# More raw weight buffers, lower priorities for two PE steps, and the attention gate block-transposed with its softmax sums as a row through DRAM

## The chip, the cores and the metric

The kernel runs on one NeuronCore of a Trainium2 chip. The metric is device time in microseconds (us) of one execution; lower is better. The engines are TensorE (PE, with its weight loads as PEld), VectorE (DVE), ScalarE (ACT), GpSimd (POOL) and SyncE (SP), which here only issues DMAs. Each engine works through its own queue in order.

## What is computed

A two-layer backbone over 256 context tokens and 2,048 latent tokens of width 1,024, in float32. Each layer normalises and modulates its input, projects it with one matrix `w_in` into the columns of three head groups, runs the groups, gates each with a SiLU path, and projects the joined result with `w_out` onto the residual. Cut to the part around the change:

```python
xn = _rms_norm(x, g_norm) * (1 + sc) + sh
(au, av, az, bq, bk, bv, bz, cq, ck, cv, co, cz, cg) = _split_proj(xn @ w_in)
...
p = softmax(einsum(q, k) * ATTN_SCALE)        # 8 query heads, 2 key heads, 64 wide
o = einsum(p, v)
y_b = o * silu(bz)                            # the gate z of group B
...
y_a = gelu(au) * (w_s @ layer_norm(gelu(av)) + b_s) * silu(az)
y_c = sigmoid(co) * rms_norm(mlstm forward + mlstm backward) * silu(cz)
x = x + gt * (concatenate([y_a, y_b, y_c]) @ w_out)
```

In the last layer only the latent tokens are put out.

## The kernel before

Tokens are cut into 18 tiles of 128 (2 context, 16 latent), `NT`. Matrix products keep float32 accuracy by splitting each operand into a rounded part and a rest (`F32R`): `split_w` (L214) does it for weights, on ACT and DVE for three chunks in four and on POOL for the fourth, and `gemm` (L223) issues three matmuls for each of the eight chunks `k` of the contraction.

The stages of a layer follow each other as `proj_phase` (L326), `attn_phase` (L1052) and `out_phase` (L229), on one SBUF stack, so that the tiles of one stage lie over the memory of the one before.

**Projection.** The 18 tiles are taken in three macros of six (`half`). For each macro the seven column groups (`groups`, L894: c1, c3, c2, a1, a2, b1, b2) are run one after the other, each over the six tiles. A group's weights are eight chunks of 128 x 512. `wload` (L969) issues their loads into 3 `raw` tiles; `wtick` (L976) splits up to two chunks into a ring of 11 `w` tiles, as far as `freed` allows, which is raised at the half and at the end of the last tile of a group. `tick` (L925) runs after each half of a tile: it advances the generators that are active (epilogues, `make_xn`, the mLSTM) and calls `wtick`. `make_xn` (L474) normalises a tile, transposes it on PE (L497), modulates and splits it; the next macro's tiles are made during the last two groups. `post_a1` (L557) is the gMLP's epilogue with the matmul by `w_s` at L591, and `post_b2` (L672) computes 2 x silu(z) as `z` and stores it to DRAM, tokens in partitions (`g_z`, L142).

**Attention.** A unit is one head and one block of four query tiles (in the first layer also one of the two context tiles), 32 units for the latents in each layer. `unit_s` (L1113) forms the scores on PE, evicts them with a running maximum on DVE (L1126) and exponentiates them on ACT, which also leaves the sums `den`. `unit_tr` (L1137) transposes the probabilities on PE and splits them, every other key tile on ACT and POOL (L1146 to L1148), the others on ACT and DVE. `unit_mm` (L1154) multiplies with the values. A value step is one key tile of a unit, 18 to a unit; the score stream runs about one unit ahead, and the value product follows the transposes by `LAG` = 5 steps.

`unit_end` (L1164) closes a unit at its last value step. For the first head of a pair it loads the gate of both heads, `sz`, with tokens in partitions. DVE takes the reciprocal of `den` (L1174), POOL scales the gate with it, a column of `sz` for each tile (L1176), ACT and DVE add the two halves of the output into `O` (L1180, L1181). At the second head PE transposes the pair's gate, four transposes (L1185), DVE multiplies `O` with it out of PSUM (L1186), and SP stores `O`. The query loads of a unit (`load_twice`, L1079) are four DMAs of pieces of 128 bytes, issued in the middle of the unit before.

**What sets the order.** The program is written out in full, and a scheduler at build time places the instructions of each engine by priority (which falls in the order of writing) in a simulated time. `late(n)` (L60) lowers the priority of what stands under it by n places, `issue_after` and `ld` (L51) order loads on SP.

Of the kernel before, what the change touches and what calls it, by code (L numbers as in the profile page):

```python
# [35 lines left out]
def hybrid_kernel(ctx: ExitStack, tc: tile.TileContext, x, c, ctxt, c_ctx, w_ada, b_ada, g_norm, w_in, w_s, b_s,  # L36
# [105 lines left out]
    g_z = [dram([P, len(b), 512], f"sz{i}") for i, b in enumerate(blocks)]  # L142
# [3 lines left out]
    g_q = [dram([len(b), P, 512], f"sq{i}") for i, b in enumerate(blocks)]  # L146
    g_k = [dram([len(b), P, P], f"sk{i}") for i, b in enumerate(blocks)]
# [178 lines left out]
    def proj_phase(l):  # L326
        with ExitStack() as st:
            xns = slots(st, half + 1, [P, 2, KC, P], "xn", F32R, "right")
            pp, xtp, rawp = (st.enter_context(tc.tile_pool(name=nm(n), bufs=b, reuse_waits="tile"))
                             for n, b in (("post", 2), ("xt", 3), ("raw", 3)))  # L330
            wring = ring(slots(st, 11, [P, 2, 512], "w", F32R))
# [142 lines left out]
            def make_xn(i, slack=True, halves=False):  # L474
# [19 lines left out]
                for b in range(2):  # L494
                    tr = ptr()
                    for k in range(4):
                        T.transpose(tr[:, k * P:(k + 1) * P], xf[:, b * 4 + k, :], ident)  # L497
                    for k in range(4):
                        kk = b * 4 + k
                        if k < 3:  # L500
                            A.activation(xf[:, kk, :], tr[:, k * P:(k + 1) * P], AF.Identity,
                                         scale=modp[l][:, s, 0, kk:kk + 1], bias=modp[l][:, s, 1, kk:kk + 1])
                        else:
                            V.tensor_scalar(xf[:, kk, :], tr[:, k * P:(k + 1) * P], modp[l][:, s, 0, kk:kk + 1],
                                            modp[l][:, s, 1, kk:kk + 1], op0=ALU.mult, op1=ALU.add)
                    bs = slice(b * 4, b * 4 + 4)
                    A.copy(slot[:, 0, bs], xf[:, bs])
                    V.tensor_tensor(slot[:, 1, bs], xf[:, bs], slot[:, 0, bs].bitcast(F32), op=ALU.subtract)
                    if b == 0 and halves:
                        yield  # L510
# [46 lines left out]
            def post_a1(i, acc, full):  # L557
# [29 lines left out]
                for gp in range(2):  # L587
                    yield
                    sv = pm()
                    for q in range(2):  # L590
                        T.matmul(sv[:, q * n:(q + 1) * n], wsT[:, 2 * gp + q, :],  # L591
                                 buf[:, 0, 2 * gp + q, j0:j1, :].rearrange("p t d -> p (t d)"),
                                 start=(q == 0), stop=(q == 1))
                    for q in range(2):
                        zz = buf[:, 1, 2 * gp + q, j0:j1, :].rearrange("p t d -> p (t d)")
                        V.scalar_tensor_tensor(zz, sv[:, q * n:(q + 1) * n], bsT[:, 2 * gp + q:2 * gp + q + 1], zz,
                                               op0=ALU.add, op1=ALU.mult)
# [74 lines left out]
            def post_b2(i, acc, full):  # L672
# [4 lines left out]
                ld(part(g_z, i), z)  # L677
# [291 lines left out]
            def wload():  # L969
                while len(wraw) < len(chunks) and len(wraw) < len(wt) + 3:  # L970
# [5 lines left out]
            def wtick(most=2):  # L976
                for _ in range(most):
                    j = len(wt)
                    if j >= len(chunks) or j >= freed[0] + 11:
                        break  # L980
# [29 lines left out]
            for mi, mac in enumerate(macros):  # L1010
                for gi, (gn, cols) in enumerate(groups):
# [8 lines left out]
                    for ii, i in enumerate(mac):  # L1020
                        full = not (last and i < NCT)
                        ml = mi == NM - 1 and (gi >= 3 or gi == 2 and ii >= 1)
                        if i in todo:
                            acc = pacc()
                            c0, w = (0, n) if full or gn == "c3" else (256, 256)
                            for hf in range(2):
                                gemm(acc, xs[i], ws, c0, w, range(hf * KC // 2, (hf + 1) * KC // 2))
                                if i == todo[-1]:
                                    freed[0] = base + (hf + 1) * KC // 2
                                tick(ml)  # L1030
                                if i == todo[-1]:
                                    wtick()
                            spawn(post[gn](i, acc, full))
# [6 lines left out]
                        if mi + 1 < NM:  # L1040
                            if gi == len(groups) - 2 and ii == half - 2:
                                spawn(make_xn(macros[mi + 1][0]))
                            if gi == len(groups) - 1 and ii + 1 < half:
                                spawn(make_xn(macros[mi + 1][ii + 1]))
# [7 lines left out]
    def attn_phase(l):  # L1052
        last = l == DEPTH - 1
        with ExitStack() as st:
# [109 lines left out]
            def unit_end(u):  # L1164
# [4 lines left out]
                if q == 0:  # L1169
                    sz = pt([P, 4, P], "sz", 3)  # L1170
                    ld(sz[:, 0:n], g_z[b][:, :, u['h'] * HD:(u['h'] + 2) * HD])
                    pairs[b] = sz, pt([P, 512], "O", 3)
                sz, O = pairs[b]
                V.reciprocal(u['den'][:, 0:n], u['den'][:, 0:n])  # L1174
                for j in range(n):
                    G.tensor_scalar(sz[:, j, q * HD:(q + 1) * HD], sz[:, j, q * HD:(q + 1) * HD],  # L1176
                                    u['den'][:, j:j + 1], 0.5, op0=ALU.mult, op1=ALU.mult)
                r = slice(q * 64, q * 64 + 64)
                rx = slice(64 - q * 64, 128 - q * 64)
                A.copy(O[r, 0:w], u['o'][rx, 0:w])  # L1180
                V.tensor_tensor(O[r, 0:w], u['o'][r, 0:w], O[r, 0:w], op=ALU.add)  # L1181
                if q == 1:
                    tr = ptr()
                    for j in range(n):
                        T.transpose(tr[:, j * P:(j + 1) * P], sz[:, j, :], ident)  # L1185
                    V.tensor_tensor(O[:, 0:w], tr[:, 0:w], O[:, 0:w], op=ALU.mult)  # L1186
# [43 lines left out]
            pend = []  # L1230
            sgen = s_stream()
# [26 lines left out]
            def flush(k):  # L1258
                while len(pend) > k:
                    u, s, t = pend.pop(0)  # L1260
                    unit_mm(u, s, t)
                    if s == u['nk'] - 1:
                        unit_end(u)
# [9 lines left out]
            flush(0)  # L1273

# [43 lines left out]
```

## Time and profile before

| | us |
|---|---|
| median of 3 runs | 3688.44 |
| lowest and highest of them | 3686.83, 3696.19 |
| the profiled execution, its own time | 3695.58 |
| its span, first to last instruction | 3693.9 |
| mean granted PE clock, share of full speed | 0.987 |

The runs differ by up to 9 us. The profile is of a single execution: its rows add up to its span of 3693.9 us, with 1.7 us around it, and that execution took 7.1 us more than the median. The stages are, roughly and overlapping: first projection to 905 us, first attention to 1,745, first output projection to 1,945, second projection to 2,690, second attention to 3,510, second output projection to the end. "Busy" of PE counts matmuls from issue to a modelled end, and they overlap. A wait names the engine and line that ended it.

### The profile page before, as it was taken

Reading aid. Unit: us, or ns where it says so; the run is one execution under the profiler, and the core shown is the slowest. Engines: PE = TensorE matmul, PEld = TensorE weight load, DVE = VectorE, ACT = ScalarE, POOL = GpSimd, SP = SyncE. Lnnn points to the kernel's source line nnn. Section 1 sums busy time; section 2 is a strip of 40 time slices with the busy share of each in tenths; the row PEclk is TensorE's granted clock in tenths of the full one; section 3 lists DMA queues with packets and bytes.
Section 4 is the critical chain, followed back from the end, with each engine's and each line's share of the span. In section 5 each row is a group of like instructions: output and inputs, shape, how many; then the busy total and the mean of one; then the engine's idle time right before and its main releaser. Section 6 shows DMA issues by size and latency. Waiting matters only on the chain. (4 is left out here: it accounts for less than half of the span.)

```text
span 3693.9 us, 58457 instructions
## 1 busy us (share of the span) xinstructions
PE 3591.9 (97%) x19405; PEld 2937.9 (80%) x19405; DVE 2564.0 (69%) x6375; ACT 1941.6 (53%) x3443; POOL 1884.4 (51%) x2448
## 2 busy tenths in 40 slices
PE   8999999998999999999999999999999999999999
PEld 4877778776888888887788788877778888888787
DVE  4676664777888888887434636467788888888754
ACT  4223243234877787776114432432368777878621
POOL 2241342453777777776432524245457777777610
PEclk9999999999999999999999999999899999999999
DMA  6446445576111011102645453557710111100143
GB/s 207 137 143 177 138 133 135 167 195 141 26 28 36 14 44 37 24 13 91 181 123 146 130 147 87 139 146 191 172 46 18 29 29 41 30 21 12 58 147 113
DMA packets 567156, 359.20 MB, mean 97 GB/s; under 512 B 348611, under 2 KB 469179, under 8 KB 566853
## 3 DMA queue, kind: packets, MB, share of 16 engines
q1 hardware_dynamic: 553636, 336.04, 34.2%
q0 software_dynamic: 2848, 9.91, 0.8%
q10 hardware_dynamic: 10368, 9.52, 0.8%
q8 instruction: 153, 2.51, 0.3%
q14 instruction: 151, 1.23, 0.1%
HBM read 269.56 MB, written 85.76 MB: 96 GB/s over the span
## 5 line engine op out<-in xcount | busy, mean ns | idle before, releaser
L226 PE MATMUL acc<-w,xn 128*128 128x512 f32 (+2 forms) x4728 | 1097.8, 386 | 7.3 <-ACT w L216 4.5
L226 PEld LDWEIGHTS acc<-w,xn 128*128 128x128 f32 x4728 | 844.8, 191 | 187.4 <-ACT w L216 6.0
L1126 DVE TENSOR_SCALAR_CACHE_REDUCE e<-acc,rqall 128x512 f32<-128x512 f32 (+1 forms) x1296 | 857.0, 688 | 150.3 <-PE acc L1124 86.2
L1159 PE MATMUL m<-pT,vst 128*128 128x512 f32 (+1 forms) x2336 | 775.8, 415 | 3.6 <-POOL pT L1148 3.2
L1124 PE MATMUL acc<-kst,qs 128*128 128x512 f32 (+1 forms) x2592 | 745.9, 385 | 8.2 <-DVE e L1126 7.2
L1148 POOL TENSOR_TENSOR pT<-pf,pT 128x512 fp32r<-128x512 f32 (+1 forms) x564 | 730.0, 1302 | 28.6
L1132 ACT ACTIVATE e<-e,nmx 128x2304 f32<-128x2304 f32 (+1 forms) x272 | 578.2, 2126 | 57.1 <-DVE nmx L1131 56.2
L1147 POOL TENSOR_SCALAR pT<-pf 128x512 fp32r<-128x512 f32 (+1 forms) x564 | 354.0, 632 | 355.8 <-ACT pf L1146 335.6
L1124 PEld LDWEIGHTS acc<-kst,qs 128*128 128x128 f32 x2592 | 446.6, 189 | 86.8 <-DVE e L1126 23.8
L1159 PEld LDWEIGHTS m<-pT,vst 128*128 128x128 f32 x2336 | 412.5, 189 | 66.3 <-POOL pT L1148 9.0
L1141 PE MATMUL tr<-ident,e 128*128 128x128 f32 x3084 | 457.0, 273 | 4.1 <-DVE pT L1151 3.4
L1141 PEld LDWEIGHTS tr<-ident,e 128*128 128x128 f32 x3084 | 373.8, 140 | 81.9 <-DVE pT L1151 6.5
L217 DVE TENSOR_TENSOR w<-raw,w 128x512 fp32r<-128x512 f32 (+1 forms) x276 | 208.1, 765 | 192.1 <-ACT w L216 188.2
L216 ACT CAST w<-raw 128x512 fp32r<-128x512 f32 (+1 forms) x276 | 160.6, 594 | 287.3 <-DMA raw<-in_w_in_dram 259.9
L1151 DVE TENSOR_TENSOR pT<-tr,pT 128x512 fp32r<-128x512 f32 x405 | 273.2, 681 | 52.5 <-ACT pT L1150 51.2
L226 PE MATMUL acc<-w,xs 128*128 128x512 f32 x1224 | 293.3, 397 | 0.6 <-DVE xs L270 0.6
L1150 ACT CAST pT<-tr 128x512 fp32r<-128x512 f32 x405 | 233.6, 586 | 96.8 <-PE tr L1141 82.5
L226 PEld LDWEIGHTS acc<-w,xs 128*128 128x128 f32 x1224 | 229.6, 188 | 57.1 <-DVE xs L270 0.9
L226 PE MATMUL x<-w,xn 128*128 128x512 f32 (+1 forms) x1128 | 263.0, 380 | 10.1 <-ACT w L216 5.5
L1146 ACT COPY pf<-tr 128x512 f32<-128x512 f32 (+1 forms) x372 | 214.3, 584 | 89.5 <-PE tr L1141 76.5
L219 POOL TENSOR_SCALAR w<-raw 128x512 fp32r<-128x512 f32 (+1 forms) x92 | 66.2, 720 | 350.1 <-PE acc L226 148.7
L226 PEld LDWEIGHTS x<-w,xn 128*128 128x128 f32 x1128 | 200.1, 190 | 55.7 <-ACT w L216 7.6
(282 smaller groups left out, 4405.5 us busy)
## 6 DMA issues: line engine op xcount, KB each, us to landing
raw<-in_w_in_dram SPq DMA_DIRECT2D x240, 256.0 KB
raw<-in_w_in_dram SPq DMA_DIRECT2D x144, 128.0 KB
mkv<-sc SPq DMA_DIRECT2D x68, 258.0 KB
xt<-snm SPq DMA_DIRECT2D x68, 256.0 KB
mst<-in_w_ada_dram SPq DMA_DIRECT2D x64, 256.0 KB
qd<-sq SPq DMA_DIRECT2D x256, 64.0 KB
xres<-xnew POOLq DMA_DIRECT2D x18, 512.0 KB, 4.0
xt<-xres SPq DMA_DIRECT2D x18, 512.0 KB
```

The costliest lines, as they stand in the source:

```text
L217: V.tensor_tensor(wt[:, 1, :n], raw[:, :n], wt[:, 0, :n].bitcast(F32), op=ALU.subtract)
L226: T.matmul(acc[:, :n], xs[:, a, k, :], ws[k][:, b, c0:c0 + n], start=(k == 0 and j == 0), stop=(k == KC - 1 and j == 2))
L1124: T.matmul(acc[:, 0:w], u['qs'][:, r, j * P:(j + 1) * P], kf[:, c0:c0 + w], start=(r == 0), stop=(r == 1))
L1126: V.tensor_scalar(e[:, c0:c0 + w], acc[:, 0:w], rqall[:, u['tiles'][j], u['h']:u['h'] + 1], None, op0=ALU.mult, op1=ALU.max, accum_out=mx[ ...
L1132: A.activation(e[:, 0:nk], e[:, 0:nk], AF.Exp, bias=nmx, scale=1.0, accum_out=u['den'][:, j:j + 1])
L1141: T.transpose(tr[:, j * P:(j + 1) * P], u['e'][j][:, s * P:(s + 1) * P], ident)
L1146: A.copy(pf[:, 0:w], tr[:, 0:w])
L1147: G.tensor_scalar(pt_[:, 0, 0:w], pf[:, 0:w], 1.0, 0.0, op0=ALU.mult, op1=ALU.add)
L1148: G.tensor_tensor(pt_[:, 1, 0:w], pf[:, 0:w], pt_[:, 0, 0:w].bitcast(F32), op=ALU.subtract)
L1150: A.copy(pt_[:, 0, 0:w], tr[:, 0:w])
L1151: V.tensor_tensor(pt_[:, 1, 0:w], tr[:, 0:w], pt_[:, 0, 0:w].bitcast(F32), op=ALU.subtract)
L1159: T.matmul(u['o'][:, 0:w], vst[u['g']][:, s, :], pt_[:, r, 0:w], start=(s == 0 and r == 0), stop=(s == u['nk'] - 1 and r == 1))
```

## The change

- In the projection there are 6 `raw` tiles instead of 3, and the ring of split weights has 10 instead of 11. `gemm` is called for each `k` by itself; on the last tile of a group `freed` rises and `wtick` is called after every `k`, while `tick` stays at two calls for a tile.
- The PE transposes of `make_xn` for the next macro and the matmuls of the gMLP are written under `late`, 60 places lower.
- `post_b2` transposes `z` on DVE in blocks of 32 x 32 before it stores it, and `g_z` takes the layout that queries already have. `unit_end` loads the pair's gate from there in four DMAs with channels in partitions, so that the PE transposes and their PSUM bank are not used.
- POOL doubles `den`, DVE takes the reciprocal, and SP stores it to DRAM, each value a piece of 4 bytes. Seven value steps later SP reads it back as a row, repeated over 64 partitions (`rd`); five steps later POOL multiplies the gate with it. `unit_end` becomes a generator which is advanced at each value step; what is left at the end of the stage runs there.

```diff
--- before.py
+++ after.py
...
     where = {t: (bi, j) for bi, b in enumerate(blocks) for j, t in enumerate(b)}
-    g_z = [dram([P, len(b), 512], f"sz{i}") for i, b in enumerate(blocks)]
     g_v = [dram([P, len(b), 128], f"sv{i}") for i, b in enumerate(blocks)]
...
     g_q = [dram([len(b), P, 512], f"sq{i}") for i, b in enumerate(blocks)]
+    g_z = [dram([len(b), P, 512], f"sz{i}") for i, b in enumerate(blocks)]
+
+    s_den = [[dram([1, len(b) * P], f"sden{i}_{h}") for h in range(8)] for i, b in enumerate(blocks)]
     g_k = [dram([len(b), P, P], f"sk{i}") for i, b in enumerate(blocks)]
...
             pp, xtp, rawp = (st.enter_context(tc.tile_pool(name=nm(n), bufs=b, reuse_waits="tile"))
-                             for n, b in (("post", 2), ("xt", 3), ("raw", 3)))
-            wring = ring(slots(st, 11, [P, 2, 512], "w", F32R))
+                             for n, b in (("post", 2), ("xt", 3), ("raw", 6)))
+            wring = ring(slots(st, 10, [P, 2, 512], "w", F32R))
...
-            def make_xn(i, slack=True, halves=False):
+            def make_xn(i, slack=True, halves=False, behind=False):
                 s = 1 if i < NCT else 0
...
                     tr = ptr()
-                    for k in range(4):
-                        T.transpose(tr[:, k * P:(k + 1) * P], xf[:, b * 4 + k, :], ident)
+                    with late(60 if behind else 0):
+                        for k in range(4):
+                            T.transpose(tr[:, k * P:(k + 1) * P], xf[:, b * 4 + k, :], ident)
                     for k in range(4):
...
                     sv = pm()
-                    for q in range(2):
-                        T.matmul(sv[:, q * n:(q + 1) * n], wsT[:, 2 * gp + q, :],
-                                 buf[:, 0, 2 * gp + q, j0:j1, :].rearrange("p t d -> p (t d)"),
-                                 start=(q == 0), stop=(q == 1))
+                    with late():
+                        for q in range(2):
+                            T.matmul(sv[:, q * n:(q + 1) * n], wsT[:, 2 * gp + q, :],
+                                     buf[:, 0, 2 * gp + q, j0:j1, :].rearrange("p t d -> p (t d)"),
+                                     start=(q == 0), stop=(q == 1))
                     for q in range(2):
...
                 V.scalar_tensor_tensor(z, th, 1.0, acc, op0=ALU.add, op1=ALU.mult)
-                ld(part(g_z, i), z)
+                V.transpose(th, z)
+                ld(row(g_z, i), th)
                 yield
...
             def wload():
-                while len(wraw) < len(chunks) and len(wraw) < len(wt) + 3:
+                while len(wraw) < len(chunks) and len(wraw) < len(wt) + 6:
                     raw = rawp.tile([P, 512], F32, tag="raw", name=nm("raw"))
...
                     j = len(wt)
-                    if j >= len(chunks) or j >= freed[0] + 11:
+                    if j >= len(chunks) or j >= freed[0] + 10:
                         break
...
                             c0, w = (0, n) if full or gn == "c3" else (256, 256)
-                            for hf in range(2):
-                                gemm(acc, xs[i], ws, c0, w, range(hf * KC // 2, (hf + 1) * KC // 2))
+                            for k in range(KC):
+                                gemm(acc, xs[i], ws, c0, w, [k])
                                 if i == todo[-1]:
-                                    freed[0] = base + (hf + 1) * KC // 2
-                                tick(ml)
-                                if i == todo[-1]:
+                                    freed[0] = base + k + 1
                                     wtick()
+                                if k % 4 == 3:
+                                    tick(ml)
                             spawn(post[gn](i, acc, full))
...
                             if gi == len(groups) - 2 and ii == half - 2:
-                                spawn(make_xn(macros[mi + 1][0]))
+                                spawn(make_xn(macros[mi + 1][0], behind=True))
                             if gi == len(groups) - 1 and ii + 1 < half:
-                                spawn(make_xn(macros[mi + 1][ii + 1]))
+                                spawn(make_xn(macros[mi + 1][ii + 1], behind=True))
                         if mi == 0 and gi == 1 and ii == 0 and fill:
...
                 if q == 0:
-                    sz = pt([P, 4, P], "sz", 3)
-                    ld(sz[:, 0:n], g_z[b][:, :, u['h'] * HD:(u['h'] + 2) * HD])
-                    pairs[b] = sz, pt([P, 512], "O", 3)
-                sz, O = pairs[b]
-                V.reciprocal(u['den'][:, 0:n], u['den'][:, 0:n])
-                for j in range(n):
-                    G.tensor_scalar(sz[:, j, q * HD:(q + 1) * HD], sz[:, j, q * HD:(q + 1) * HD],
-                                    u['den'][:, j:j + 1], 0.5, op0=ALU.mult, op1=ALU.mult)
+                    z = pt([P, 512], "z", 3)
+                    zv = g_z[b].rearrange("j (a r) (b c) -> r b (j a) c", a=4, c=32)
+                    for k in range(4):
+                        ld(z[k * 32:k * 32 + 32, 0:w].rearrange("r (a c) -> r a c", c=32), zv[:, 2 * u['h'] + k])
+                    pairs[b] = z, pt([P, 512], "O", 3), pt([P, 512], "rd", 2)
+                z, O, rd = pairs[b]
                 r = slice(q * 64, q * 64 + 64)
                 rx = slice(64 - q * 64, 128 - q * 64)
+                G.tensor_scalar(u['den'][:, 0:n], u['den'][:, 0:n], 2.0, None, op0=ALU.mult)
+                V.reciprocal(u['den'][:, 0:n], u['den'][:, 0:n])
+                ld(s_den[b][u['h']].rearrange("o (j p) -> (o p) j", p=P), u['den'][:, 0:n])
                 A.copy(O[r, 0:w], u['o'][rx, 0:w])
                 V.tensor_tensor(O[r, 0:w], u['o'][r, 0:w], O[r, 0:w], op=ALU.add)
+                for _ in range(7):
+                    yield
+                ld(rd[r, 0:w], s_den[b][u['h']].to_broadcast([64, w]))
+                for _ in range(5):
+                    yield
+                G.tensor_tensor(z[r, 0:w], z[r, 0:w], rd[r, 0:w], op=ALU.mult)
                 if q == 1:
-                    tr = ptr()
-                    for j in range(n):
-                        T.transpose(tr[:, j * P:(j + 1) * P], sz[:, j, :], ident)
-                    V.tensor_tensor(O[:, 0:w], tr[:, 0:w], O[:, 0:w], op=ALU.mult)
+                    V.tensor_tensor(O[:, 0:w], z[:, 0:w], O[:, 0:w], op=ALU.mult)
                     ld(g_y[b][:, u['h'] // 2], O[:, 0:w].rearrange("p (a t) -> p a t", a=n))
...
             pend = []
+            ends = []
             sgen = s_stream()
...
                     if s == u['nk'] - 1:
-                        unit_end(u)
+                        ends.append(unit_end(u))
+                    for end in list(ends):
+                        if next(end, 0) is not None:
+                            ends.remove(end)
...
             flush(0)
+            for end in ends:
+                for _ in end:
+                    pass
...
     for l in range(DEPTH):
```

## Rows read from the trace of the kernel before

**Rows 1.** The page's part 1: busy time, share and instructions of each engine.

```profile
PE 3591.9 (97%) x19405; PEld 2937.9 (80%) x19405; DVE 2564.0 (69%) x6375; ACT 1941.6 (53%) x3443; POOL 1884.4 (51%) x2448
```

**Rows 2.** Stretches: us, busy us of PE, PEld, DVE, ACT, POOL, clock, DMA, GB/s.

```profile
1000.00:1700.00 700.00, 696.82 (x4177) 587.90 (x4176) 590.76 (x1614) 551.21 (x810) 512.44 (x622) 1.00 0.12 27
2750.00:3450.00 700.00, 699.09 (x4206) 594.15 (x4205) 584.98 (x1600) 553.11 (x790) 512.07 (x620) 1.00 0.12 25
90.00:850.00 760.00, 726.90 (x3751) 588.70 (x3749) 493.49 (x1146) 243.22 (x591) 290.41 (x405) 0.98 0.55 154
```

**Rows 3.** Waits of PE over the whole span: total us, times, longest.

```profile
PE tr L497 <- DVE xt L504: 9.1, 6, 1.8
...
PE x L226 <- ACT w L216: 5.5, 5, 3.8
...
PE acc L226 <- ACT w L216: 4.5, 3, 2.4
...
PE m L1159 <- POOL pT L1148: 3.2, 5, 1.7
...
PE x L226 <- POOL w L220: 2.2, 2, 1.7
PE x L226 <- DVE O L1186: 2.2, 1, 2.2
PE x L226 <- DVE w L217: 2.0, 2, 1.4
...
PE m L591 <- DVE asv L577: 1.8, 2, 1.4
```

**Rows 4.** Groups by line, PE: the gate's transposes (busy us, mean ns | idle before).

```profile
L1185 PE MATMUL tr<-ident,sz 128*128 128x128 f32 x96 | 14.7, 272 | 0.0
...
L1185 PE MATMUL x<-ident,sz 128*128 128x128 f32 x40 | 6.0, 272 | 0.0
```

**Rows 5.** Timeline: four gate transposes in a row (start us, us).

```profile
977.49 0.60 PE L1185 MATMUL tr<-ident,sz 128*128 128x128 f32 x4
```

**Rows 6.** Groups by line, POOL and DVE: operations nearest to the new ones.

```profile
L1176 POOL TENSOR_SCALAR sz<-sz,den 128x64 f32<-128x64 f32 x272 | 83.0, 327 | 61.6 <-DVE den L1174 57.3 <-PE acc L1124 1.9 <-DMA sz<-sz 1.2
...
L669 DVE STREAM_TRANSPOSE k<-k 128x512 f32<-128x512 f32 x34 | 23.9, 704 | 28.7 <-POOL k L627 28.6
...
L1095 POOL TENSOR_TENSOR kst<-qd,kst 64x512 fp32r<-64x512 f32 x6 | 8.0, 1332 | 7.2 <-ACT kst L1094 5.9 <-issue 1.3
```

**Rows 7.** SP's issues by tile, gate and queries (ns min/median/max).

```profile
L53 SPq DMA_DIRECT2D sz<-sz x36: 523/524/630, 908.5 to 3367.6; - x36
...
L53 SPq DMA_DIRECT2D qd<-sq x288: 302/486/2411, 866.3 to 3349.9; - x144
```

**Rows 8.** Timeline: last piece of a query load, and its first use.

```profile
869.58 0.62 SPq L53 DMA_DIRECT2D qd<-sq  x1
...
872.07 0.62 ACT L1108 CAST qs<-qd 128x512 fp32r<-128x512 f32 x1 [3.34 <-DMA qd<-sq]
```

**Rows 9.** Chain that ended last: a broadcast load in a busy stretch.

```profile
2437.85 5.29 DMA xt<-snm
```

**Rows 10.** Timeline: splits and raw loads ahead of the longest wait for w.

```profile
303.61 1.12 ACT L216 CAST w<-raw 128x512 fp32r<-128x512 f32 x2
...
305.25 2.54 SPq L53 DMA_DIRECT2D raw<-in_w_in_dram  x4
...
308.12 0.62 ACT L216 CAST w<-raw 128x512 fp32r<-128x512 f32 x1 [2.86 <-DMA raw<-in_w_in_dram]
```

**Rows 11.** Chain that ended last: 24 matmuls of one tile and group.

```profile
3550.39 5.62 PE x L226 x24
```

**Rows 12.** Waits of PE, 0 to 100 us.

```profile
PE tr L497 <- DVE xt L504: 3.1, 2, 1.8
```

**Rows 13.** Timeline of SP at the start: raw and w_ada loads.

```profile
12.71 3.05 SPq L53 DMA_DIRECT2D raw<-in_w_in_dram  x3
16.85 7.57 SPq L53 DMA_DIRECT2D xn<-in_w_ada_dram  x8
```

## The prediction

> **What bounds the kernel now.** I read the page's engine line first [rows 1]: TensorE (PE) is busy for 97% of the span, the next engine for 69%. Then the table by stretch [rows 2]. In both attention stages PE is busy for 696.8 and 699.1 of 700 us, at clock 1.00, while VectorE (DVE) is at 84%, ScalarE (ACT) at 79%, GpSimd (POOL) at 73% and the DMA engines at 12%. So in attention every PE instruction that is taken away shortens the kernel, as long as no other engine is made to wait for something new. In the first layer's projection stage PE lacks 33 of 760 us. Third, the waits of PE [rows 3] say what it lacks there: split weights (w), the normalised input (L504) and the spatial gate's input (L577). The rest of its idle time belongs to the mLSTM chain, which the change leaves as it is. I count gains only where PE is the one that waits.
>
> **Part 1, attention: 136 PE transposes of the gate go.** There are 96 and 40 of them [rows 4], 272 ns each, which looks like 37 us. They are pipelined, though: four end 0.60 us after the first begins [rows 5]. One alone takes 0.272, so the other three follow at (0.60 - 0.272) / 3 = 0.109 us. What PE gets back is 136 x 0.109 = 14.9 us, all on its path. By the busy time the sum would end 22 us lower; I take the spacing. The Trainium skill, page "Trainium Kernel Development and Optimization", section "Performance Expectations", calls matmul busy time a bad metric because matmuls are pipelined, so by that rule too it is 15 and not 37; the trace agrees with its 0.60 us for four of 0.27.
>
> POOL loses 272 scalings, 83 us busy [rows 6]. It gains 72 products of 64x512, nearest row the 64x512 subtraction of 1.332 us, = 96 us [rows 6], and 72 small den x 2, nearest row the scaling again, = 24 us. Net +37 us over some 1,600 us of attention (64 units of 25 us, below), 73% to 75%: hidden under PE. DVE does as many operations as before; its last product reads SBUF where it read PSUM, and I count 0. What is new on DVE is a wait: the reciprocal now follows a POOL operation, and the evictions L1126, on which PE waits, are queued behind it. At worst each of 72 waits lasts one long POOL operation, 1.332 us: 96 us of DVE time, 84% to 90%. At best nothing, since the exponentials that den needs end about a unit (25 us) earlier than the value product does. PE is covered by its accumulator banks; I take 0 and keep 0 to +30 us (a third of it reaching PE).
>
> SyncE's queue (SP): per pair of heads the one gate load of 0.52 us becomes four like the query loads, 0.49 us each, plus two stores and two loads, some 4 us more per pair [rows 7]. A pair lasts about 50 us (a unit has 40 score and 36 value matmuls, 72 transposes and 2 for the gate, 150 in all; 4,206 in 700 us [rows 2] make 25 us a unit), so the queue has room, and a query load is issued half a unit (12 us) ahead. The store waits for the reciprocal and the row's read for the store; behind both on SP stand the next query loads, which those 12 us cover. The value steps are 18 to a unit, 1.4 us each. The reciprocal's row is read 7 steps (9.7 us) after the store and multiplied 5 steps (6.9 us) later. From below, a load lands within 2.5 us of its issue: the last piece of a query load is issued at 869.58 and used at 872.07 [rows 8]. From above, a broadcast load in a busy stretch takes 5.3 us [rows 9]. Either way store plus load are 5 to 11 us of the 16.6 us they have. So 0. If the cover goes, POOL waits, and behind it stand the odd probability splits L1147 and L1148 that PE consumes.
>
> **Part 2, end of the first attention.** PE waits 2.2 us there for bank x, which the last gate transposes hold until the product L1186 has read it [rows 3]. That wait goes. What is late next is the layout: w_out tiles lie over memory of the gate, O and now rd, freed only after the copy, the sum and the product behind the last value matmul. I take -1, bounds -2 to +4.
>
> **Part 3, weights.** The waits of PE for w are 5.5 + 4.5 + 2.2 + 2.0 = 14.2 us [rows 3]; nearly all stand in the first layer. The longest is 3.8 us, and its chain is plain [rows 10]: ACT casts two of the three raw tiles at hand at 303.61 (the third is POOL's), the next four loads are issued only at 305.25, and ACT then sits 2.86 us until one lands at 308.12. With six raw tiles the loads of the next six chunks have landed by then. Against it stands one split tile less, 10 for 11, so two instead of three lie ready when the last tile of a group starts. That is more than made up where raws are the limit: the splits now follow each k of the last tile, and one chunk is consumed in 3 x 5.62 / 24 = 0.70 us [rows 11], while ACT casts two in 1.12 us [rows 10] and POOL takes every fourth. I take two thirds of 14.2: -9; bounds -14 and, if the smaller ring costs as much as the raws bring, +5.
>
> **Part 4, lower priorities.** PE waits 9.1 us for L504 in all, 3.1 of them in the start-up [rows 12], where nothing is lowered; 6.0 remain, with 1.8 for the gMLP product. A later place in PE's order lets other matmuls go ahead. It helps where such matmuls exist. I take half, -4; bounds -8 and +4, since everything else is placed anew too. The clock in those stretches is 0.98 on the mean [rows 2], so I count nothing for it.
>
> **Part 5, start-up and the new transposes.** Three more raw loads go out before the second half of w_ada: three took 3.05 us of SP, then eight w_ada loads 7.57 us [rows 13]. The modulation that the first products need comes up to 3 us later, partly repaid because more chunks lie ready. +2, bounds 0 to +3. The store of z stays one DMA per tile. The DVE transposes of z, 34 x 0.704 = 24 us [rows 6], lie in projection stages where DVE is at 65%; but they come where the splits are wanted. +1, bounds 0 to +5.
>
> **Sum.** -14.9 - 1 - 9 - 4 + 2 + 1 = -26 us. The profiled execution took 3695.6 us (span 3693.9), 7.1 above the median, so it would take 3669.7; against the median of 3688.4 that is **3662.5**, or 0.7% less. One measurement can tell about 0.3% (11 us) from no change.
>
> **Rivals.** (a) *The new handshake stalls attention* (slower). Place: POOL's product with rd and DVE's reciprocal behind POOL. For it: POOL is in order and does half of the probability splits; no row shows a store of four-byte pieces, and each of the 72 stores is 512 of them. Against it: 16.6 us of cover, and PE waited on POOL's splits for only 3.2 us in the whole run [rows 3]. It decides once store plus load exceed 16.6 us; then each us over it, on 72 units with half of it reaching PE, costs 36 us. With 1.5 us over, +54, that is 3662 + 54 = 3716; at 0.8 us over it is 3691, no change. The Trainium skill, page "DMA: Bandwidth & Descriptors", section "Rules for kernel authors", speaks against such a store: a non-contiguous last dimension becomes one descriptor per element. No run here shows it yet. Chance 0.14.
> (b) *Only the transposes pay.* The smaller ring and the new places take back what raws bring: -14.9 + 3 = 3676, on the bound between faster and same. For it: the splits for a new group still crowd into one tile's 5.6 us. Against it: the late splits waited for loads, not for slots [rows 10]. Chance 0.14.
> (c) *Projection gains all it can.* All of 14.2 and 6.0 + 1.8, and start-up free: -14.9 - 2 - 14.2 - 7.8 = -39, 3649, a little less if the clock rises with it. Chance 0.12.
> (d) *The change does not do what it says*: the raws are not loaded earlier because SP, in order, is held by other waits; weights unchanged, 3671. It stays inside the forecast's range.
> The forecast with (d) has 0.60; its own range is 3650 to 3676.
>
> **How the numbers follow.** Below 3677.4 lie the forecast (0.60), (c) (0.12) and half of (b): 0.75 with small losses taken off. Within 0.3%: the rest of (b) and the mild end of (a), 0.14. Above 3699.5: most of (a), 0.11. For 8 in 10 the range goes from (c) with some clock, 3642, to the mild end of (a), 3694.
>
> **What would show it.** Right: no L1185 on PE; in attention the same share of PE (over 99%) with as little wait on DVE e and POOL pT as now, and the two stages together some 15 us shorter; PE's waits for w under 6 us; ACT's idle time before L216 ended less by raw loads; L504's under 6 us. Wrong: POOL waiting for DMA rd, DVE den waiting for POOL in sums of tens of us, PE waits on pT grown, or PE waits for w that end on splits held by the ring rather than by loads.

## The result and the profile after

The changed kernel takes **4438.06 us** (median of 4 runs, 4429.88 to 4441.4) where the kernel before took 3690.57 on the same chip (4 runs): a ratio of 1.2014, 95% interval 1.1994 to 1.2034. Slower by 747.5 us, where 26 us less were forecast. The profiled execution took 4441.4 us (span 4439.7). Lines moved with the change: score products are L1129 (L1124 before), value products L1164 (L1159), the odd splits on POOL L1152 and L1153 (L1147 and L1148), POOL's product of gate and sums L1193, the doubling of the sums L1183, their reciprocal L1184.

The page of the kernel after, its parts 1, 2, 4 and 5 (the group's columns are busy us, mean ns, then idle time before it and what ended it); the first line answers to [rows 1]:

```profile
PE 3745.4 (84%) x19269; PEld 3048.3 (69%) x19269; DVE 2628.4 (59%) x6409; ACT 1947.9 (44%) x3443; POOL 1929.0 (43%) x2320
...
PEclk9999999878888888888999999998888888888899
...
PE acc L228 8%; DMA sden<-den 6%; PE m L1164 4%; PE acc L1129 3%; DMA rd<-sden 2%; PE x L228 2%; PE tr L1146 2%; DVE e L1131 2%; DMA xt<-snm 1%; PE x L1146 1%; POOL z L1193 1%; SPq L53 1%; DVE pT L1156 1%; POOL pT L1152 1%; DVE qs L1114 1%
...
L1193 POOL TENSOR_TENSOR z<-z,rd 64x512 f32<-64x512 f32 x72 | 86.2, 1197 | 737.4 <-DMA rd<-sden 627.4
```

No engine became the bound: PE fell from 97% to 84%. The store of the sums (sden<-den) stands second in the chain that ended last, the read of the row (rd<-sden) behind it, and POOL sat idle for 737.4 us before its 72 products of gate and sums, nearly as much as the kernel lost (747.5).

Two stretches inside the attention stages (columns as in [rows 2], whose first two lines they answer to; the second stage now lies later):

```profile
1000.00:1700.00 700.00, 524.37 (x2854) 437.59 (x2853) 416.01 (x1133) 384.82 (x578) 364.11 (x398) 0.86 0.15 25
3300.00:4000.00 700.00, 533.72 (x2905) 443.93 (x2904) 421.55 (x1112) 387.35 (x554) 369.83 (x393) 0.86 0.14 24
```

PE did 2,854 products in 700 us where it did 4,177, every other engine fell with it, and the mean granted clock went from 1.00 to 0.86, a mean of the two levels 2.4 and 1.2 GHz. The clock fell where PE idled: between 1200 and 1210 us PE was busy throughout and the clock 1.00, between 1210 and 1220 it was busy for 4.22 us and the clock 0.75, between 1220 and 1230 it was busy again and the clock still 0.91. In the runs below in which PE was busy again (the product held, both repairs, the group held) it stood at 0.99 to 1.00 in these stages. So some of the loss is the lower clock after each stall; no run tells it apart from the stall itself.

The waits after, of PE (they answer to [rows 3]), POOL and SP (total us, times, longest):

```profile
PE m L1164 <- POOL pT L1152: 380.2, 46, 10.1
PE m L1164 <- POOL pT L1153: 172.9, 32, 10.7
...
PE tr L500 <- DVE xt L507: 15.4, 10, 2.6
PE acc L228 <- POOL w L221: 13.9, 3, 6.2
...
POOL z L1193 <- DMA rd<-sden: 627.4, 59, 22.2
...
SPq L53 <- DMA sden<-den: 620.3, 69, 10.8
```

PE's waits for POOL's splits went from 3.2 us (L1148) to 553. The value products take their operands from POOL every other step; POOL, in order, sat at the product. SP sat nearly as long, 620.3 us, at the row's read, which waits for the store.

One unit in the timeline of the kernel after (start us, us, engine, line):

```profile
1199.52 0.22 POOL L1183 TENSOR_SCALAR den<-den 128x4 f32<-128x4 f32 x1 [2.45 <-ACT e L1137]
...
1200.22 0.17 DVE L1184 RECIPROCAL den<-den 128x4 f32<-128x4 f32 x1
1200.42 0.38 SPq L53 DMA_DIRECT2D sden<-den  x1
...
1209.71 0.45 SPq L53 DMA_DIRECT2D rd<-sden  x1
1214.55 1.26 POOL L1193 TENSOR_TENSOR z<-z,rd 64x512 f32<-64x512 f32 x1 [9.00 <-DMA rd<-sden]
...
1225.24 0.58 ACT L1186 COPY O<-m 64x512 f32<-64x512 f32 x1
...
1261.31 0.58 ACT L1186 COPY O<-m 64x512 f32<-64x512 f32 x1
```

Two things are to be seen. The store takes 9.29 us (1200.42 to 1209.71, where SP goes on) and the read 4.84 (to 1214.55). And POOL was ready for the product at 1205.55 (1214.55 less 9.00): only 5.1 us after the store was issued. The unit's copy of O, which in the program stands **ahead** of all the twelve value steps, comes at 1261.31, 46.8 us **after** the product. (The copy at 1225.24 closes the unit before: 274 value products have begun by then, and the eleven units ahead of this one have 268.) The doubling, which the program writes just ahead of that copy, was done 61.8 us before it, right behind the exponentials it needs. So the whole chain (doubling, reciprocal, store, read, product) was built into the engines' orders more than a unit ahead of its place in the text, and on POOL only six operations of the splits stand between doubling and product.

The DMA view of the same 17 us, 1199 to 1216, in 40 slices of 0.425 us:

```profile
GB/s 120 139 137 107 50 3 2 0 0 0 0 0 0 0 0 0 0 0 0 58 0 0 0 0 0 0 0 0 0 0 0 29 48 106 125 0 0 0 0 0
```

From slice 7 (about 1202) on nothing of the store moves any more (the one slice with 58 GB/s, at 1207.3, is two packets of instructions); SP waits until 1209.7. What is long is the landing of the store, not the moving of its 2 KB.

### The profile page after: what moved, and what is told of

Same layout as the page of the kernel before. It is cut to its first block, busy times and chain, and to the rows that moved or that the text cites. A ratio compares the mean times of both kernels' runs of the same rounds, so it can differ in the third digit from the quotient of the medians.

```text
span 4439.7 us, 58660 instructions
## 1 busy us (share of the span) xinstructions
PE 3745.4 (84%) x19269; PEld 3048.3 (69%) x19269; DVE 2628.4 (59%) x6409; ACT 1947.9 (44%) x3443; POOL 1929.0 (43%) x2320
## 5 line engine op out<-in xcount | busy, mean ns | idle before, releaser
L1164 PE MATMUL m<-pT,vst 128*128 128x512 f32 (+1 forms) x2336 | 849.8, 450 | 554.8 <-POOL pT L1152 380.2
L1164 PEld LDWEIGHTS m<-pT,vst 128*128 128x128 f32 x2336 | 456.8, 209 | 652.0 <-POOL pT L1152 396.2
L1129 PE MATMUL acc<-kst,qs 128*128 128x512 f32 (+1 forms) x2592 | 793.2, 406 | 19.7 <-DVE e L1131 19.1
L1153 POOL TENSOR_TENSOR pT<-pf,pT 128x512 fp32r<-128x512 f32 (+1 forms) x564 | 734.5, 1309 | 31.0
L1129 PEld LDWEIGHTS acc<-kst,qs 128*128 128x128 f32 x2592 | 481.7, 204 | 105.9 <-DVE e L1131 33.0
L1146 PE MATMUL tr<-ident,e 128*128 128x128 f32 x3094 | 491.6, 287 | 8.4 <-DVE pT L1156 5.0
L1152 POOL TENSOR_SCALAR pT<-pf 128x512 fp32r<-128x512 f32 (+1 forms) x564 | 359.1, 640 | 305.9 <-ACT pf L1151 299.7
L1146 PEld LDWEIGHTS tr<-ident,e 128*128 128x128 f32 x3094 | 404.8, 149 | 94.4 <-issue 11.3
L1193 POOL TENSOR_TENSOR z<-z,rd 64x512 f32<-64x512 f32 x72 | 86.2, 1197 | 737.4 <-DMA rd<-sden 627.4
L1155 ACT CAST pT<-tr 128x512 fp32r<-128x512 f32 x403 | 233.1, 584 | 301.5 <-PE tr L1146 278.3
L1156 DVE TENSOR_TENSOR pT<-tr,pT 128x512 fp32r<-128x512 f32 x403 | 272.0, 680 | 103.2 <-ACT pT L1155 102.7
L228 PE MATMUL acc<-w,xs 128*128 128x512 f32 x1224 | 298.7, 402 | 16.6 <-POOL w L221 13.9
L219 DVE TENSOR_TENSOR w<-raw,w 128x512 fp32r<-128x512 f32 (+1 forms) x276 | 223.7, 846 | 67.6 <-ACT w L218 67.1
L1146 PE MATMUL x<-ident,e 128*128 128x128 f32 x1546 | 245.9, 283 | 2.2 <-DVE pT L1156 2.0
```

Source lines behind the costliest of these rows:

```text
L219: V.tensor_tensor(wt[:, 1, :n], raw[:, :n], wt[:, 0, :n].bitcast(F32), op=ALU.subtract)
L228: T.matmul(acc[:, :n], xs[:, a, k, :], ws[k][:, b, c0:c0 + n], start=(k == 0 and j == 0), stop=(k == KC - 1 and j == 2))
L1129: T.matmul(acc[:, 0:w], u['qs'][:, r, j * P:(j + 1) * P], kf[:, c0:c0 + w], start=(r == 0), stop=(r == 1))
L1146: T.transpose(tr[:, j * P:(j + 1) * P], u['e'][j][:, s * P:(s + 1) * P], ident)
L1152: G.tensor_scalar(pt_[:, 0, 0:w], pf[:, 0:w], 1.0, 0.0, op0=ALU.mult, op1=ALU.add)
L1153: G.tensor_tensor(pt_[:, 1, 0:w], pf[:, 0:w], pt_[:, 0, 0:w].bitcast(F32), op=ALU.subtract)
```

## The experiments

**The product held.** POOL's product may not stand ahead of the last probability split traced before it; nothing else is changed.

```
+ lastp[0] = G.tensor_tensor(pt_[:, 1, 0:w], pf[:, 0:w], ...)   # the odd split
...
+ with tc.issue_after(lastp[0]):
      G.tensor_tensor(z[r, 0:w], z[r, 0:w], rd[r, 0:w], op=ALU.mult)
```

> The changed kernel, but POOL's product of the gate with rd is held behind the last POOL probability split that was written before it, so that it stands about 10 splits behind the doubling of den in POOL's order instead of 1 to 3. Nothing else is changed. Theory (order): the loss is POOL waiting in order for rd, 59 waits of 10.6 us (627 us), while PE waits 553 us for pT behind it. Then POOL's wait for rd falls under 30 us, PE's waits for pT under 15 us, and the time is 3650 to 3680 us. Rival (SP): the stores hold SP's queue for 9 us each (620 us in all) and make the other loads late; that stays, so the time stays over 4200 us. Rival (DVE behind POOL): DVE's reciprocals wait 42 us for POOL; that stays too, and at most 40 us of the loss would go with the order.

Measured: 3755.42 us (4 runs), 1.0187 [1.0165, 1.0208] of before. One edge in POOL's order gives 683 of the 747 us back. POOL waits no longer for rd, as expected, but the time lies 75 us above the expected range. SP still waits for the store: the rival of SP, which expected over 4200 us, saw that wait and had far too high a price for it. The waits of SP in this run, then a stretch of its timeline:

```profile
SPq L53 <- DMA sden<-den: 491.7, 63, 9.5
```

```profile
1161.21 0.44 SPq L53 DMA_DIRECT2D sden<-den  x1
1161.70 1.03 SPq L53 DMA_DIRECT2D qd<-sk  x2
1169.84 0.45 SPq L53 DMA_DIRECT2D rd<-sden  x1
1170.34 0.59 SPq L53 DMA_DIRECT2D qd<-sk  x1
1174.32 0.62 ACT L1099 CAST kst<-qd 128x512 fp32r<-128x512 f32 x1 [7.82 <-DMA qd<-sk]
```

The read of the row is in SP's queue, and a load of keys stands behind it. ACT, in order too, sits 7.82 us at the cast of that load; between 1150 and 1250 PE waits 5.1 us for ACT's splits L1155 and 7.0 for DVE's L1156, which follow them.

**The projection parts alone**, with the gate as it was before (three raw tiles to six, ring of 11 to 10, splits after each k, lower priorities):

> The projection parts alone: 6 raw tiles, ring of 10, splits after each k, lowered priorities; gate and end of unit as before the change. Theory (order): all of the loss is in attention, so this gains what parts 3 to 5 of the prediction say without the new DVE transposes: -9 - 4 + 2 = -11 us, 3679 us, between 3668 and 3690; PE's waits for w under 4 us instead of 14.2. Rival (projection loses too): the smaller ring or the new places cost, 3700 us or more, and the pinned kernel then stays over 3690.

Measured: 3688.09 us (10 runs), 1.0002 [0.9989, 1.0016]: nothing. Its waits of PE:

```profile
PE tr L499 <- DVE xt L506: 11.0, 10, 2.5
...
PE acc L227 <- DVE w L218: 3.3, 1, 3.3
...
PE x L227 <- DVE w L218: 2.1, 1, 2.1
```

The waits for w fell from 14.2 [rows 3] to 5.4 us (with those under 1 us, from 15.6 to 6.3): not under 4 as this run expected, but by the 9 us of the prediction's part 3, and the time stayed. Those for the normalised input, which the lower priorities were to shorten, rose from 9.1 to 11.0.

**The store in 128 pieces of 16 bytes**, the order left as the change has it; the row then holds the sums in another order:

```
- ld(s_den[b][u['h']].rearrange("o (j p) -> (o p) j", p=P), u['den'][:, 0:n])
+ ld(s_den[b][u['h']].rearrange("o (p j) -> (o p) j", p=P), u['den'][:, 0:n])
```

> The changed kernel with one edit: the store of den writes the 4 values of a partition side by side (128 pieces of 16 bytes instead of 512 of 4 bytes); rd is read as before and so holds the sums in another order. Order in POOL as in the changed kernel. Theory (small pieces make the store slow): SP's wait from store to read falls from 9 to about 3 us, POOL's wait for rd from 10.6 to about 5 us each, and the time to 3900 to 4150 us. Rival (the latency is that of any store to DRAM that is read back): the wait stays 8 to 10 us and the time 4400 us or more.

**The store in 512 pieces of 4 bytes, each 64 bytes from the next**; the row is read from the start of that space and so doesn't hold the sums:

```
...
+ ld(s_den[b][u['h']].rearrange("o (j p s) -> (o p) j s", p=P, s=16)[:, :, 0], u['den'][:, 0:n])
...
```

> The changed kernel with 512 pieces of 4 bytes still, but each 64 bytes from the next (40 stores of 32 KB at the start lay the memory out); rd reads the first values of that memory, so it does not hold the sums. Theory (neighbouring pieces are slow because they share memory lines): the store takes about 3 us as with 16-byte pieces, 3900 to 4150 us. Rival (a piece of 4 bytes is slow by itself): 9 us as in the changed kernel, 4400 us or more.

Measured: 3764.36 and 3754.93 us (one run each), far below the 3900 us that both expected at the least. Waits of POOL and SP, first with 16 bytes:

```profile
POOL z L1193 <- DMA rd<-sden: 103.8, 56, 4.3
...
SPq L53 <- DMA sden<-den: 90.3, 68, 4.3
```

then with 4 bytes set apart:

```profile
POOL z L1197 <- DMA rd<-sden: 82.5, 50, 3.7
...
SPq L53 <- DMA sden<-den: 88.3, 69, 3.0
```

SP's wait falls from 9.0 us a time (620.3 / 69) to 1.3 in both. As many pieces as before, of the same size, cost nothing if they are apart: it is not the number of pieces, nor that they have 4 bytes, but that neighbours of 4 bytes are written next to each other. Units of half the pieces (8 of the 72 have only two tiles) say the same: in the kernel after a store of 256 pieces took 8.82 us (1066.46 to 1075.28), one of 512 took 9.29. And with 128 pieces each, in the first of these two runs, a store of 16-byte pieces let SP go on after 1.50 us (945.33 to 946.83), one of 8-byte pieces, with half the bytes, after 2.95 (954.27 to 957.22). Whether the pieces hold each other up because they share a line of the memory, as the expectation has it, no run shows.

**Both repairs**: the product held and 16-byte pieces, the row read back in its right order by a strided view on POOL.

> The change with both repairs at once: POOL's product with rd held behind the last probability split, and the store of the sums as 128 pieces of 16 bytes. My theory (two holds: POOL behind rd, and SP behind the sums' store, which delays the next loads) expects both to be gone: POOL's wait for rd under 20 us, SP's for the store under 100 us in all, the attention stretch 2750 to 3450 at 699 of 700 us or more, and the time near 3688 (attention -15, the change's other parts about 0 as measured, the wait of the first output stage for split weights +6, some us at the edges of the attention stages): 3675 to 3695. The rival, that the 67 us left with the product held are not SP's, expects 3740 to 3760 again.

**The same gate on the projection code of before:**

> The gate's part alone, with both repairs, on the projection code of before (no more raw buffers, no smaller ring, no lower priorities). If the projection parts are worth nothing also beside the new gate, as they were beside the old one, it takes the same as the run with everything and both repairs, within 10 us, 3675 to 3695. If they pay only beside the new gate (PE then free to use earlier weights), it is 10 to 20 us slower than that one.

Measured: 3701.80 us (10 runs, 1.0023 [1.0010, 1.0035]) and 3687.44 us (10 runs, 0.9989 [0.9978, 1.0001]). So the two waits are additive only in part:

| | product where the order put it | product held |
|---|---|---|
| pieces of 4 bytes side by side | 4438 | 3755 |
| pieces of 16 bytes | 3764 (one run) | 3702 |

The runs of the table were made on different chips, whose times of the kernel before differ by up to 3 us. Either repair ends most of POOL's stall; the second one then takes away 54 to 63 us more. The rival that the 67 us left in the first experiment were not SP's has fallen. The first of these two lies 7 us above its range: the change's other parts cost 14 us beside the new gate, which neither side of the second expectation had. And in neither did the attention give its 15 us: by the marks below, its two stages last 842.6 and 824.1 us in the gate's part alone, for 845.4 and 824.9 before. The end of the first, in the timeline of PE in the gate's part alone:

```profile
1733.88 1.40 PE L1162 MATMUL m<-pT,vst 128*128 128x512 f32 x5
1735.12 4.13 PE L228 MATMUL x<-w,xs 128*128 128x512 f32 x17
1739.09 0.40 PE L1162 MATMUL m<-pT,vst 128*128 128x512 f32 x1
1739.33 0.85 PE L228 MATMUL x<-w,xs 128*128 128x512 f32 x3
1740.02 0.39 PE L1162 MATMUL m<-pT,vst 128*128 128x512 f32 x1
1740.24 1.10 PE L228 MATMUL x<-w,xs 128*128 128x512 f32 x4
1747.59 8.02 PE L228 MATMUL acc<-w,xs 128*128 128x512 f32 x24 [6.24 <-POOL w L221]
```

The same place in the kernel before:

```profile
1741.75 2.15 PE L1159 MATMUL m<-pT,vst 128*128 128x512 f32 x7
1746.11 5.84 PE L226 MATMUL x<-w,xs 128*128 128x512 f32 x24 [2.21 <-DVE O L1186]
```

Bank x, which the gate's transposes used to hold, is free, so 20 products of the next stage now go ahead of the last two value products. All that waits for the end of the attention (its memory, into which the next weights are split) comes later, and PE then waits 6.24 us for a weight.

**That group held behind the last value product:**

```
+ if ti < 2 and turn["acc"] % 4 == 0:        # the first groups on bank x
+     with tc.issue_after(lastmm[0]):
+         gemm(acc, xs, ws[g], 0, 512)
...
```

> The gate's part with both repairs, and on PE the first group of the output stage that uses bank x held behind the last value product. In the gate's part alone 20 matmuls of that group stand ahead of the last two value products (4.1 us of them), since no transposes of the gate hold the bank any more; the end of the attention, and with it the memory of the split weights, comes 4 to 5 us later, and PE then waits 6.2 us for weights. If that is the cause, the wait falls to about 2 to 3 us and the kernel takes 3 to 6 us less than the gate's part alone (3682 to 3685 beside a before of 3691). If the late weights have another cause (the stores and loads on SP), the time stays at 3687.

Measured: **3675.03 us** (5 runs, 3671.46 to 3675.96), 0.9951 [0.9938, 0.9964]: faster than both kernels, 18.4 us (0.5%) below before. The same place in its timeline:

```profile
1732.08 5.76 PE L230 MATMUL x<-w,xs 128*128 128x512 f32 x24
1739.54 1.20 PE L230 MATMUL acc<-w,xs 128*128 128x512 f32 x4 [1.71 <-POOL w L223]
1741.23 4.93 PE L230 MATMUL acc<-w,xs 128*128 128x512 f32 x20 [0.49 <-POOL w L224]
```

The wait of 6.24 has become 1.71 and 0.49, and the stage's third group starts 8.1 us earlier; by 3.8 of these the execution was ahead already, so the place itself gave 4.3, as expected. The gain in the median, 12 us between two chips or 14 when each is taken against the before of its chip, is larger than the 3 to 6 expected. The hold acts at the end of the second attention too, which the expectation left out: 20 products stood ahead there as well (from 3504.64), and the lead of the profiled execution grows from 13.3 us (3503.39 against 3490.09) to 15.5 at the end of the span. The rest lies in the two projection stages (5.2 us ahead of the first attention), where PE's order is the same as in the gate's part alone but for a few products of the mLSTM that changed places. Single executions of that one lie 14 us apart (3683.27 to 3697.27); where the rest comes from is open.

**The projection parts beside this gate, one at a time**, first raws, ring and splits after each k, then the lower priorities:

> The run before plus the change's six raw tiles, ring of ten and splits after every k. The kernel with all of the change and both repairs took 14 us more than the gate's part alone; if the raws and the smaller ring are what costs, this one takes 10 to 16 us more than the run before; if the lower priorities do, 0 to 3 more; if the two only cost together, 3 to 8.

> The run with the held group plus the change's lower priorities alone. If these are what costs beside the new gate, it takes 10 to 16 us more than the run with the held group; if the raws do, 0 to 3 more or less.

Measured: 3686.46 us (10 runs, 0.9981 [0.9969, 0.9993]), 11 more than without; and 3701.97 us (10 runs, 1.0028 [1.0017, 1.0038]), 27 more. Neither expectation allowed for both. They don't add up either: together they cost 14 beside the gate's part alone (without the held group), and 0 beside the old gate. The waits of PE in the run with lower priorities:

```profile
PE tr L506 <- DVE xt L513: 11.1, 8, 2.9
...
PE x L230 <- ACT w L220: 7.7, 4, 6.0
```

They were 7.4 and 6.2 (longest 3.9) without. The marks of the stages (profiled executions, us; first score product and last value product of each attention):

| | first score | last value | first score | last value | span |
|---|---|---|---|---|---|
| before | 898.5 | 1743.9 | 2689.9 | 3514.8 | 3693.9 |
| projection parts alone | 884.6 | 1735.1 | 2679.1 | 3504.9 | 3683.7 |
| all, both repairs | 888.7 | 1742.6 | 2687.1 | 3517.2 | 3694.7 |
| gate alone, both repairs | 897.8 | 1740.4 | 2685.8 | 3509.9 | 3687.0 |
| gate alone, both repairs, and the group held | 892.6 | 1732.2 | 2671.6 | 3493.0 | 3671.5 |
| group held, and raws, ring | 885.6 | 1733.9 | 2672.5 | 3500.8 | 3679.3 |
| group held, and lower priorities | 902.1 | 1745.8 | 2688.8 | 3513.4 | 3691.9 |

Wherever the raws come early, the first score product does too (7 to 14 us), and the first attention then lasts longer: 850.5 us for 845.4 beside the old gate, 848.3 for 839.6 beside the new one. A likely reason, not tested: its first products run beside the end of the recurrent (mLSTM) chain, which did not end earlier by as much.

## Why the prediction was wrong

**Part 1, the step that failed: "store plus load are 5 to 11 us of the 16.6 us they have".** Both numbers in it were wrong, and either of them, had it held, would have spared most of the loss, as the table of four shows.

The 16.6 us were 12 value steps counted in the program's text. The order on each engine is made afterwards from what is ready and urgent, and it drew the chain forward until POOL had 5.1 us between the store's issue and the product. I had read from the trace that the sums are ready a unit early, and used it to excuse the reciprocal's wait; the same fact lets the whole chain move up and its cover go.

The bound from above for store and load was taken from a broadcast load of 5.3 us [rows 9]; it bounded the load of the unit shown (4.84) but not the store, for which the trace of before had no row like it. The store of 9.29 us was nearly four times the load's row that stood for it from below (2.5 us, [rows 8]). 14.1 us of store and load less 5.1 of cover are the 9.0 us for which POOL sits.

Rival (a) had the mechanism, with too small a price. It put half of POOL's stall on PE; here POOL's 717.8 us (627.4 for rd and 90.4 that the view leaves without a releaser, 10.0 a unit) cost 683, what holding the product gave back (the clock's return included). POOL does every second split, and a late split holds the value products of all. And its condition, over 16.6 us, was not met in the unit shown: 14.1 was enough. The other half of that handshake, the reciprocal behind POOL, cost little: DVE waited 42.4 us for it in the whole run (13 waits), and 8.5 with both repairs.

The Trainium skill, page "DMA: Bandwidth & Descriptors", section "Rules for kernel authors", was right to speak against this store, but the reason it gives, a descriptor for each element, is not what cost here: 512 pieces set apart have as many and took 1.3 us of waiting. The same page, section "Anatomy of one DMA — SWDGE (gpsimd) path", gives about 2 us for the fixed part of a DMA that GpSimd issues, most of it the receipt of the write. These stores are issued by SP; the traces have about as much for 16-byte pieces (2.27 us from store to read at 944.71 in the gate's part alone) and far more, 9.29, for pieces of 4 bytes side by side.

**SP: "behind both on SP stand the next query loads, which those 12 us cover".** The cover held for queries and failed for the key loads, which the preparation of the next half issues just in time. It was the second stall: the store's landing cost 54 us with the product held (3755 to 3702). ACT's waits for key loads fell with it from 33.3 to 8.4 us; how the rest reached PE was not traced.

**The transposes: 14.9 us.** Too low, if anything, by one execution of each kernel. The sums of O in the second attention, before and in the gate's part alone, 28 units apart:

```profile
2765.99 0.70 DVE L1181 TENSOR_TENSOR O<-m,O 64x512 f32<-64x512 f32 x1
...
3468.15 0.69 DVE L1181 TENSOR_TENSOR O<-m,O 64x512 f32<-64x512 f32 x1 [0.40 <-ACT O L1180]
```

```profile
2764.01 0.69 DVE L1186 TENSOR_TENSOR O<-m,O 64x512 f32<-64x512 f32 x1 [0.28 <-ACT O L1185]
...
3456.73 0.69 DVE L1186 TENSOR_TENSOR O<-m,O 64x512 f32<-64x512 f32 x1 [0.27 <-ACT O L1185]
```

702.16 us became 692.72: 9.44 us for 56 transposes, 0.17 each, nearer to the busy time that the view by line gives (20.7 us for 136, [rows 4]) than to my 0.109. The steady part of the attention gained; its edges gave most of it back: from the last of these sums to the last value product there were 46.7 us before and 53.2 with the new gate.

**Part 2: -1, bounds -2 to +4.** The wait for bank x did go, and with it the brake that kept the next stage behind the last value products: "what is late next" was the right question, and the layout half of the answer. Of the 6.24 us wait, the overtaking was the part that could be cured.

**Part 3: -9.** The waits for w fell by about 9 us as worked out, and the time did not: the attention behind them started earlier and lasted longer. I had counted a wait of PE as time, without asking what PE would meet at the end of the stage. **Part 4: -4.** Wrong in sign: the waits for the input rose beside the old gate (9.1 to 11.0) and beside the new (7.4 to 11.1). **Part 5** could not be told from scatter.

Without the two stalls the gate's part alone should have taken about 15 us less than before (parts 1 and 2 and the transposes of z). It took 4.4 less in the first form (3687.44 against 3691.82) and 18.4 less with the group held.

## What to carry to other kernels

Where a planner orders the engines, a distance in the program's text is no distance in time: if a step must not come early on an in-order engine, hold it by an edge, and read the cover of a round trip from the built order. The tiny store through DRAM was priced by its landing here: give each partition one run of 16 bytes rather than 4-byte neighbours from different partitions, and look at what stands behind its wait on the issuing queue. And when a wait disappears, ask what it was holding back: here the bank's wait kept the next stage's products off the end of this one.

## What the runs showed of the hardware

Neighbouring pieces of 4 bytes from different partitions made a store of 2 KB land after 9.29 us, 256 of them after 8.82, though none of its data moved in the last 7 us; pieces of 8 bytes side by side landed after 2.95 us where 16-byte pieces took 1.50; the same 4-byte pieces 64 bytes apart, or pieces of 16 bytes, made SP wait 1.3 us a time instead of 9.0. What holds the landing back was not tried further. Reading the row through a strided view made POOL's product slower (a mean of 1,496 ns with the group held, for 1,258 with the product held and both operands in order).
